# Five edits in the scan of a bidirectional RWKV-7 layer, with a new written order

## The chip, the cores and the metric

One core of a Trainium2 chip. TensorE (PE in the profile; PEld its weight loads), VectorE (DVE), ScalarE (ACT), GpSimd (POOL) and SyncE (SP, which issues the DMAs) run side by side and wait for one another through semaphores. The metric is the device time of one execution in microseconds; lower is better. The time of the kernel before is the median of three runs.

## The reference

A trunk of two layers on 512 tokens of 1024 channels. A layer is: half-step SwiGLU feed-forward, token mixer, half-step feed-forward, each followed by a layer norm. Layer 0 mixes with a neighbourhood attention; layer 1 with the bidirectional RWKV-7 mixing, the only part that the change touches:

```python
def step(state, inp):
    r_t, w_t, k_t, v_t, a_t, b_t = inp
    sa = jnp.einsum('zbhij,zbhj->zbhi', state, a_t)
    state = state * w_t[..., None, :] + sa[..., None] * b_t[..., None, :] + v_t[..., None] * k_t[..., None, :]
    return state, jnp.einsum('zbhij,zbhj->zbhi', state, r_t)

_, ys = lax.scan(step, jnp.zeros((2, B, H, N, N), f32), xs)
y = (ys[:, 0] + ys[::-1, 1]).transpose(1, 0, 2, 3)
mu = jnp.mean(y, axis=-1, keepdims=True)
var = jnp.mean(jnp.square(y - mu), axis=-1, keepdims=True)
y = ((y - mu) * lax.rsqrt(var + RW_GN_EPS)).reshape(B, S, D) * lnx_g + lnx_b
```

There are 16 heads of 64 channels (N), and two directions z, one scan each. `w` is a decay, `a` and `b` come from the normalised keys and a learned rate, `r` reads the state out. After the scan y is normalised per head, a bonus is added, it is gated and multiplied by the output matrix.

## The kernel before, in words

The two feed-forwards of layer 0, its attention and the first feed-forward of layer 1 run first, then the projections of RWKV-7, then the scan (from about 1385 to 1800 us of the profile), then the last feed-forward. All of it outside the scan is the same in both kernels.

The scan handles a *pair* of heads (128 channels, `hp` 0 to 7) at a time, and cuts the 512 tokens into eight chunks of 64. Within a chunk the recurrence becomes matrix products; a small triangular system per chunk, direction and head has to be inverted; and a *chain* of eight steps carries the 64x64 state from chunk to chunk. A *slot* n runs the chain of pair n, and beside it the preparation of the pairs n+1 to n+3 and the end of pair n-1. Each job is a generator with a one-letter name, the *threads* of `slot`, and the strings of the table `SEQ` say which thread goes on next; slots 0 to 4 share one string. The threads that matter here:

- `f0`, `f1`: `front`, one per direction. Prefix sums of the log decay (`lw` with `tri`), the exponentials `e` and `e2`, the rate `th` (a matmul of `ah` with `a2r`), and from them the factors `ar` and `bk`.
- `g0`, `g1`: `grams`, the products of `bk` and `ar` inside a chunk, masked into `xs`; ScalarE copies pieces into `qd` and `qc`, and DMAs put `ar` into `az` and `xs`. A call multiplies four chunks of two heads.
- `t0`, `t1`: `tails`, `bk` transposed to `tb`.
- `v`: `values`, eight products of the value weights `wv` with `xraw`. There is one `wv` buffer; `weigh` asks for the next pair's 512 KB when the last of the eight is issued.
- `n`: `turn`, the values transposed to tokens by rows (`vt`), once forward and once reversed.
- `i`, `k`, `j`: `invert`, `inverted`, `merge`. `invert` transposes `qd` into `qs` on VectorE and solves 31 rows of a 32x32 triangular system on GpSimd, two operations a row (`tm`, `zs`), from row 31 to row 1. `inverted` transposes the result on VectorE and sends it to `az` in eight DMAs; `merge` joins the 32x32 blocks on PE (32x32 tiles).
- `c`, `d`: `chain` (`c<-vt,xs`, `y<-vt,az`, `c<-wr,az`, `m<-vt,tb` on PE, copies on ScalarE, the decay on VectorE) and `outputs` (`y<-vt,xs`).
- `x`, `e`: `finish` (mean, variance and normalisation of y on VectorE) and `gate` (loads `bon` and `gate`, transposes y, bonus and gate on VectorE).
- `o`: `outs`, in slots 5 to 7: the first five blocks of the output product, with weights that lie in buffers of the scan that have come free (`bk`, `ar`, `az`, `wv`, `xs`).

`k.bank(tag)` takes a PSUM bank of a group: two each of `a` and `g`, one each of `p`, `c`, `m` and `y`. `wide` splits a product into two of 64 output rows. PE, ScalarE and VectorE issue in the order of the table (`manual_schedule(engines=MANUAL_SCAN)`); SP's and GpSimd's order is found by a scheduler from a model of time. In the profile an fp32 matmul is two records, a transpose one.

Of the kernel before, what the change touches and what calls it, by code (L numbers as in the profile page):

```python
# [10 lines left out]
F32 = mybir.dt.float32  # L11
# [1098 lines left out]
class Scan:  # L1110
# [13 lines left out]
    def begin(self, g2):  # L1124
# [10 lines left out]
        self.first.update(zip(("e", "e2", "th"), (ring[:, i * S : (i + 1) * S] for i in range(3))))  # L1135
# [9 lines left out]
    def open(self, pool):  # L1145

        self.pool = pool
# [3 lines left out]
        self.onesb = early.tile([P, P], F32, name="onesb")  # L1151
        unit = lambda i: (pool.tile([P, 2, 2, 4, CH], F32, name=f"xs{i}"), pool.tile([P, 2, 4, CH], F32, name=f"tb{i}"))
        units = {i: unit(i) for i in (2, 4, 3)}
        for n in ("e", "e2", "th"):
            self.place(n, [P, S], 2)
# [33 lines left out]
    def receptances(self):  # L1189
# [58 lines left out]
    def run(self, late, lead, ln):  # L1248
        with self.k.tc.manual_schedule(engines=MANUAL_SCAN):
            self.zs, self.rs, self.out = [], self.receptances(), self.outs()  # L1250
            next(self.rs)
            self.led, self.stored = [], 0
            for n in range(-2, HEADS // 2):
                if n == HEADS // 2 - 1:
                    self.early.tile([P, 56], F32, name="pad")
                    self.opened.close()
                    late.enter_context(self.k.early())
                    self.lw = self.leads(lead, ln)
                self.slot(n)
            self.ending = self.finish(HEADS // 2 - 1)  # L1260
            next(self.ending)
# [78 lines left out]
    def load(self, hp):  # L1340
# [12 lines left out]
        p.units, p.ar, p.bk = [], [], []  # L1353
# [14 lines left out]
    def front(self, hp, z):  # L1368
# [14 lines left out]
        e = tile_("e", [P, S], 2)  # L1383
        nc.scalar.activation(e, pi, AF.Exp)
# [3 lines left out]
        pa = k.bank("a")  # L1388
        self.wide(pa, p.a2[:, z, :], self.ah, True, True)
        th = tile_("th", [P, S], 2)  # L1390
        nc.scalar.activation(th, pa, AF.Tanh, scale=0.5, bias=k.col(C_A0H + z, hp))
# [15 lines left out]
        nc.vector.tensor_tensor(rt, chunks(p.r), ec, ALU.mult)  # L1407
# [18 lines left out]
    def grams(self, hp, z):  # L1426
# [5 lines left out]
        for q in range(2):  # L1432
# [4 lines left out]
            for j in range(4):  # L1437
                for h, hs in enumerate(HALF):
                    nc.tensor.matmul(pgs[h][:, j * P : (j + 1) * P], flat(bk[hs, q * 4 + j]), ar[hs, :, q * 4 + j],  # L1439
                                     start=True, stop=True)  # L1440
# [71 lines left out]
    def turn(self, hp):  # L1512
# [4 lines left out]
        for z, zs in enumerate(HALF):  # L1517
            nc.vector.memset(p.vt[zs, 0, z], 0.0)
# [3 lines left out]
        for z in range(2):  # L1522
            pv = k.bank("p")
            for t in range(NT):
                nc.tensor.transpose(pv[:, t * P : (t + 1) * P], (vr if z else p.v)[:, t * P : (t + 1) * P], k.ident)
# [8 lines left out]
    def invert(self, hp):  # L1534
# [6 lines left out]
        for s in range(31, 0, -1):  # L1541
            c0 = s // 2
            n = 16 - c0
            tm = tile_("tm", [P, 256])
            tv = tm[:, : s * n].rearrange("p (a b) -> p a b", b=n)
            nc.gpsimd.tensor_tensor(tv, qs[:, s, 0:s].rearrange("p (a o) -> p a o", o=1).broadcast_to([P, s, n]),  # L1546
                                    zs[:, s : s + 1, c0:].broadcast_to([P, s, n]), ALU.mult)
            nc.gpsimd.tensor_tensor(zs[:, 0:s, c0:], zs[:, 0:s, c0:], tv, ALU.add)  # L1548
# [44 lines left out]
    def chain(self, hp):  # L1593
# [3 lines left out]
        vt = p.vt  # L1597
# [298 lines left out]
```

## Time and profile before

| what | us |
|---|---|
| median of three runs | 2185.55 (2181.95 to 2185.77) |
| the profiled execution, its own time | 2179.1 |
| its span, first to last instruction | 2177.3 |
| PE busy | 2138.7 (98%) |
| GpSimd busy | 1392.8 (64%) |
| VectorE busy | 1052.1 (48%) |
| ScalarE busy | 954.7 (44%) |

The shares are means over stages that differ. A busy PE says little, since a matmul's record lasts until its result is written and records overlap; what tells is how far apart matmuls start, and for what PE waits. The mean granted clock of the span is 0.996 of full speed.

### The profile page before, as it was taken

Reading aid. Unit: us, or ns where it says so; the run is one execution under the profiler, and the core shown is the slowest. Engines: PE = TensorE matmul, PEld = TensorE weight load, DVE = VectorE, ACT = ScalarE, POOL = GpSimd, SP = SyncE. Lnnn points to the kernel's source line nnn. Section 1 sums busy time; section 2 is a strip of 40 time slices with the busy share of each in tenths; the row PEclk is TensorE's granted clock in tenths of the full one; section 3 lists DMA queues with packets and bytes.
Section 4 is the critical chain, followed back from the end, with each engine's and each line's share of the span. In section 5 each row is a group of like instructions: output and inputs, shape, how many; then the busy total and the mean of one; then the engine's idle time right before and its main releaser. Section 6 shows DMA issues by size and latency. Waiting matters only on the chain.

```text
span 2177.3 us, 35335 instructions
## 1 busy us (share of the span) xinstructions
PE 2138.7 (98%) x13952; PEld 1686.0 (77%) x13952; DVE 1052.1 (48%) x1526; ACT 954.7 (44%) x1675; POOL 1392.8 (64%) x1226
## 2 busy tenths in 40 slices
PE   9999999999999999999999999999999999999998
PEld 8888888888888888888888877446666568888876
DVE  3223355377333333553333569636888554333345
ACT  3333345377333333453333444537777434333333
POOL 5988855555478778578888543046767614877753
PEclk9999999999999999999999999999999999999999
DMA  6444462332244444544444553853444552444443
GB/s 210 150 155 144 142 230 97 116 114 76 91 162 140 141 145 136 212 141 142 144 137 144 198 175 125 288 172 104 133 122 128 165 190 83 150 135 141 140 165 126
DMA packets 145366, 321.47 MB, mean 148 GB/s; under 512 B 31056, under 2 KB 51152, under 8 KB 145200
## 3 DMA queue, kind: packets, MB, share of 16 engines
q1 hardware_dynamic: 145200, 319.21, 45.0%
q8 instruction: 110, 1.80, 0.3%
q14 instruction: 56, 0.46, 0.1%
HBM read 261.22 MB, written 45.88 MB: 141 GB/s over the span
## 4 chain that ended last, share of the span: by engine, by line
PE 91%; DMA 3%; DVE 2%; ACT 1%; issue 1%; POOL 1%; SPq 0%; DVEq 0%; ACTq 0%; POOLq 0%
PE bank L287 17%; PE bank L286 17%; PE bank L288 17%; PE bank L923 17%; PE a L1115 5%; PE bank L349 4%; PE g L1439 1%; PE y L1115 1%; DMA wv<-in_w_rv_dram 1%; PE bank L1306 1%; PE m L1115 1%; PE bank L677 1%; PE y L1614 1%; PE c L1607 1%; PE y L1637 1%
## 5 line engine op out<-in xcount | busy, mean ns | idle before, releaser
L277 POOL TENSOR_TENSOR w<-raw,w 128x1024 fp32r<-128x1024 f32 x198 | 485.7, 2455 | 224.4 <-ACT w L276 216.9
L286 PE MATMUL bank<-xT,w 128*128 128x512 f32 x1264 | 493.4, 390 | 0.0
L287 PE MATMUL bank<-xT,w 128*128 128x512 f32 x1264 | 492.3, 389 | 0.0
L288 PE MATMUL bank<-xT,w 128*128 128x512 f32 x1264 | 491.9, 389 | 0.0
L276 ACT ACTIVATE w<-raw 128x1024 fp32r<-128x1024 f32 x202 | 213.0, 1058 | 312.9 <-POOL ts L894 123.1
L493 DVE SCALAR_TENSOR_TENSOR ar<-bank,tmp 128x512 f32<-128x512 f32 x88 | 60.9, 692 | 570.3 <-PE bank L288 560.2
L288 PEld LDWEIGHTS bank<-xT,w 128*128 128x128 f32 x1264 | 237.3, 188 | 49.9
L286 PEld LDWEIGHTS bank<-xT,w 128*128 128x128 f32 x1264 | 237.3, 188 | 48.6
L287 PEld LDWEIGHTS bank<-xT,w 128*128 128x128 f32 x1264 | 237.4, 188 | 48.2
L923 PE MATMUL bank<-wx,an 128*128 128x512 f32 x792 | 187.5, 389 | 0.0
L923 PEld LDWEIGHTS bank<-wx,an 128*128 128x128 f32 x792 | 148.7, 188 | 31.2
L923 PE MATMUL bank<-w,ring 128*128 128x512 f32 x720 | 168.8, 390 | 1.9 <-POOL w L277 1.7
L277 POOL TENSOR_TENSOR wx<-ra,wx 128x512 fp32r<-128x512 f32 x132 | 167.0, 1291 | 3.1 <-ACT wx L276 3.1
L277 DVE TENSOR_TENSOR ring<-ar,ring 128x1024 fp32r<-128x1024 f32 x44 | 122.5, 2785 | 87.7 <-ACT ring L276 87.6
L923 PEld LDWEIGHTS bank<-w,ring 128*128 128x128 f32 x720 | 134.9, 188 | 31.1 <-POOL w L277 2.7
L491 ACT ACTIVATE tmp<-bank 128x512 f32<-128x512 f32 x88 | 52.6, 597 | 233.4 <-PE bank L288 233.2
L1546 POOL TENSOR_TENSOR tm<-qs,zs 128x126 f32<-128x126 f32 (+22 forms) x248 | 103.6, 418 | 79.3 <-issue 35.8
L1548 POOL TENSOR_TENSOR zs<-zs,tm 128x126 f32<-128x126 f32 (+22 forms) x248 | 110.9, 447 | 19.4
L276 ACT ACTIVATE wx<-ra 128x512 fp32r<-128x512 f32 x132 | 82.7, 632 | 79.3 <-PE bank L923 66.3
L277 POOL TENSOR_TENSOR ring<-raw,ring 128x1024 fp32r<-128x1024 f32 x24 | 60.1, 2515 | 78.8 <-ACT ring L276 78.8
L277 POOL TENSOR_TENSOR w<-xT,w 128x1024 fp32r<-128x1024 f32 x25 | 62.7, 2511 | 45.2 <-ACT w L276 45.2
L499 DVE TENSOR_TENSOR ar<-ar 128x256 f32<-128x256 f32 x44 | 90.3, 2052 | 1.5
(346 smaller groups left out, 3946.3 us busy)
## 6 DMA issues: line engine op xcount, KB each, us to landing
raw<-in_ffn_w_in_dram SPq DMA_DIRECT2D x176, 512.0 KB, 3.5
ra<-in_ffn_w_out_dram SPq DMA_DIRECT2D x44, 1024.0 KB, 4.9
xT<-d_late SPq DMA_DIRECT2D x29, 512.0 KB, 5.0
xT<-in_ffn_w_out_dram SPq DMA_DIRECT2D x23, 512.0 KB, 4.6
d_late<-ts SPq DMA_DIRECT2D x44, 256.0 KB, 3.0
d_late<-ra SPq DMA_DIRECT2D x44, 256.0 KB, 2.0
raw<-in_w_qkv_dram SPq DMA_DIRECT2D x16, 512.0 KB, 3.6
raw<-in_ffn_w_out_dram SPq DMA_DIRECT2D x12, 512.0 KB, 3.6
```

The costliest lines, as they stand in the source:

```text
L276: self.hi = self.nc.scalar.activation(h, raw, AF.Copy).ins
L277: self.lo = (eng or self.nc.vector).tensor_tensor(l, raw, h.bitcast(F32), ALU.subtract).ins
L286: nc.tensor.matmul(out, wh, xh, start=start, stop=False)
L287: nc.tensor.matmul(out, wh, xl, start=False, stop=False)
L288: nc.tensor.matmul(out, wl, xh, start=False, stop=stop)
L349: nc.tensor.matmul(acc[t, h], a, u[:, i, h * 512 : (h + 1) * 512], start=first and n == 0, stop=last and n == 2)
L493: nc.vector.scalar_tensor_tensor(raw[:, 3:7:3] if j else raw[:, 0:8:7], halves_of(pu), 0.5, halves_of(s), ALU.mult, ALU.mult)
L499: nc.vector.tensor_tensor(a(2), a(1), a(0), ALU.subtract)
L923: self.nc.tensor.matmul(acc, lhs, u[:, i], start=bool(first) and m == 0, stop=last and m == 2, skip_group_check=more)
L1115: self.nc.tensor.matmul(out[hs], w[:, hs], x, start=start, stop=stop)
L1546: nc.gpsimd.tensor_tensor(tv, qs[:, s, 0:s].rearrange("p (a o) -> p a o", o=1).broadcast_to([P, s, n]), zs[:, s : s + 1, c0:].broadcast_to ...
L1548: nc.gpsimd.tensor_tensor(zs[:, 0:s, c0:], zs[:, 0:s, c0:], tv, ALU.add)
```

## The change

- *Written DMA order.* From slot 0 on, SP also issues in the order in which the code asks, as the other three do; the strings of slots 0 to 7 are new.
- *Last rows on VectorE.* `invert` solves rows 31 to 5 on GpSimd; `inverted` solves rows 4 to 1 on VectorE (tile `tn`) before its transpose.
- *Values centred as they are turned.* `turn` multiplies by `centre`, the identity less 1/64 within each head, in place of a transpose. Every v has then mean zero over its head, so y has too, and `finish` drops the mean and its subtraction.
- *Both rates at once.* `front` of direction 0 makes the rates of both directions (pairs 1 to 7), each from the 64 rows of `a2r` that are not zero, on four 64x64 tiles of the array, the second into bank `p`.
- *Grams as 64x64.* A gram matmul of 64 rows and 128 columns of weights becomes two of 64 columns. In chunk 0 of the chain, whose state is zero, `c` uses the 64 rows that hold values, `y<-vt,az` is left out, and the memsets of `vt` go.
- `e` gets a column of ones on each side of a chunk (`es`), so that one operation makes `ar` in place of two.

```diff
--- before
+++ after
        "t0 v f0 v v b f0 v t1 i f0 t1 f0 v n v r b",
-    0: "x v c n g0 c c f1 f1 c v d c c c x f1 c v x c d c c v f1 c l f0 g0 f1 x c l c g0 c n v c f1 f0 g0 c d c "
-       "c n g0 d c x d g1 c g0 e g1 x c c g1 g1 v g1 c v d f1 g1 i c k t0 t0 c c k b f0 t1 t1 j c v f0 d f0 c v "
-       "c c j d f0 b",
...
+    0: "n c v x g0 c c x n c d c c c f1 x c l x f1 v c d c f1 c f1 n c f0 f1 x c g0 c c g0 g0 v c f1 v g0 c d c "
+       "c d f1 g1 c v f0 e g0 g1 t0 c c g1 b g1 c v c g1 g1 l v k i c t0 c c k f0 v c f0 v j b c t1 t1 x c c j d "
+       "d d d f0 f0",
...
 }
...
 GATES = 4
+ROWS_DVE = 4
 START_TAGS = ("k0", "iv0", "r0", "lw", "kz0", "ar0", "bk0", "a2r", "pcs")
...
         self.onesb = early.tile([P, P], F32, name="onesb")
+        self.centre = early.tile([P, P], F32, name="centre")
...
+        es = [pool.tile([P, NC, CH + 2], F32, name=f"es{i}") for i in range(2)]
+        for e in es:
+            nc.gpsimd.memset(e[:, :, 0 :: CH + 1], 1.0)
+        self.es += es * (HEADS // 2)
...
             nc.sync.dma_start(getattr(self, n), self.consts[n])
+        nc.vector.scalar_tensor_tensor(self.centre, self.onesb, -1.0 / HD, self.k.ident, ALU.mult, ALU.add)
         chunk(0)
...
     def run(self, late, lead, ln):
+        self.zs, self.rs, self.out = [], self.receptances(), self.outs()
+        self.led, self.stored = [], 0
         with self.k.tc.manual_schedule(engines=MANUAL_SCAN):
-            self.zs, self.rs, self.out = [], self.receptances(), self.outs()
             next(self.rs)
-            self.led, self.stored = [], 0
-            for n in range(-2, HEADS // 2):
+            for n in range(-2, 0):
+                self.slot(n)
+        with self.k.tc.manual_schedule(engines=MANUAL_SCAN | {mybir.EngineType.SP}):
+            for n in range(HEADS // 2):
                 if n == HEADS // 2 - 1:
...
         yield
-        e = tile_("e", [P, S], 2)
-        nc.scalar.activation(e, pi, AF.Exp)
+        ew = self.es.pop(0)
+        e = ew[:, :, 1 : CH + 1]
+        nc.scalar.activation(e, chunks(pi), AF.Exp)
         e2 = tile_("e2", [P, S], 2)
...
         yield
-        pa = k.bank("a")
-        self.wide(pa, p.a2[:, z, :], self.ah, True, True)
-        th = tile_("th", [P, S], 2)
-        nc.scalar.activation(th, pa, AF.Tanh, scale=0.5, bias=k.col(C_A0H + z, hp))
+        ways = (z,) if hp == 0 else range(2) if z == 0 else ()
+        pas = {i: k.bank("ap"[i] if len(ways) > 1 else "a") for i in ways}
+        for hs in HALF:
+            for i, pa in pas.items():
+                nc.tensor.matmul(pa[hs], p.a2[HALF[i], i, hs], self.ah[HALF[i]], start=True, stop=True)
+        for i, pa in pas.items():
+            p.th[i] = tile_("th", [P, S], 3)
+            nc.scalar.activation(p.th[i], pa, AF.Tanh, scale=0.5, bias=k.col(C_A0H + i, hp))
+        th = p.th[z]
         ar, bk = tile_(f"ar{z}", [P, 2, NC, CH]), tile_(f"bk{z}", [P, NC, 2, CH])
...
         bt, kt = bk[:, way, z, way], bk[:, way, 1 - z, way]
-        kc, ec = chunks(p.k), chunks(e)
-        if z == 0:
-            a1, a0, k1, k0, e1 = at[:, :, 1:], at[:, :, 0:1], kc[:, :, 1:], kc[:, :, 0:1], ec[:, :, : CH - 1]
-        else:
-            a1, a0, k1, k0, e1 = at[:, :, : 0 : -1], at[:, :, 0:1], kc[:, :, : CH - 1], kc[:, :, CH - 1 :], ec[:, :, 1:]
-        nc.vector.scalar_tensor_tensor(a1, k1, k.col(C_NKK, hp), e1, ALU.mult, ALU.mult)
-        nc.vector.tensor_scalar(a0, k0, k.col(C_NKK, hp), None, ALU.mult)
+        nc.vector.scalar_tensor_tensor(at[:, :, way], chunks(p.k), k.col(C_NKK, hp), ew[:, :, 2 * z : 2 * z + CH], ALU.mult, ALU.mult)
         end = 0 if z else CH - 1
-        ends = ec[:, way, end : end + 1]
+        ends = e[:, way, end : end + 1]
         for h in range(2):
...
         yield
-        nc.vector.tensor_tensor(rt, chunks(p.r), ec, ALU.mult)
+        nc.vector.tensor_tensor(rt, chunks(p.r), e, ALU.mult)
         if z == 0:
...
             for j in range(4):
-                for h, hs in enumerate(HALF):
-                    nc.tensor.matmul(pgs[h][:, j * P : (j + 1) * P], flat(bk[hs, q * 4 + j]), ar[hs, :, q * 4 + j],
-                                     start=True, stop=True)
+                for i, rows in enumerate(HALF):
+                    for h, hs in enumerate(HALF):
+                        nc.tensor.matmul(pgs[h][rows, j * P : (j + 1) * P], bk[hs, q * 4 + j, i], ar[hs, :, q * 4 + j],
+                                         start=True, stop=True)
...
         p.vt = tile_("vt", [P, NC, 2, 2, CH], 2)
-        for z, zs in enumerate(HALF):
-            nc.vector.memset(p.vt[zs, 0, z], 0.0)
         vr = tile_("vr", [P, S])
...
             for t in range(NT):
-                nc.tensor.transpose(pv[:, t * P : (t + 1) * P], (vr if z else p.v)[:, t * P : (t + 1) * P], k.ident)
+                self.wide(pv[:, t * P : (t + 1) * P], (vr if z else p.v)[:, t * P : (t + 1) * P], self.centre, True, True)
             for j in range(2):
...
         zs = self.zs.pop(0)
-        for s in range(31, 0, -1):
-            c0 = s // 2
-            n = 16 - c0
-            tm = tile_("tm", [P, 256])
-            tv = tm[:, : s * n].rearrange("p (a b) -> p a b", b=n)
-            nc.gpsimd.tensor_tensor(tv, qs[:, s, 0:s].rearrange("p (a o) -> p a o", o=1).broadcast_to([P, s, n]),
-                                    zs[:, s : s + 1, c0:].broadcast_to([P, s, n]), ALU.mult)
-            nc.gpsimd.tensor_tensor(zs[:, 0:s, c0:], zs[:, 0:s, c0:], tv, ALU.add)
         p.zs, p.qs = zs, qs
-        yield
+        for s in range(31, ROWS_DVE, -1):
+            self.eliminate(nc.gpsimd, p, s, tile_("tm", [P, 256]))
+        yield
+
+    def eliminate(self, eng, p, s, tm):
+
+        zs, qs = p.zs, p.qs
+        c0 = s // 2
+        n = 16 - c0
+        tv = tm[:, : s * n].rearrange("p (a b) -> p a b", b=n)
+        eng.tensor_tensor(tv, qs[:, s, 0:s].rearrange("p (a o) -> p a o", o=1).broadcast_to([P, s, n]),
+                          zs[:, s : s + 1, c0:].broadcast_to([P, s, n]), ALU.mult)
+        eng.tensor_tensor(zs[:, 0:s, c0:], zs[:, 0:s, c0:], tv, ALU.add)
...
         p = self.st[hp]
+        for s in range(ROWS_DVE, 0, -1):
+            self.eliminate(nc.vector, p, s, self.tile("tn", [P, 64]))
         zs, qs = p.zs, p.qs
...
         p = self.st[hp]
-        vt = p.vt
+        p.written, vt = False, p.vt
         self.py[hp] = k.bank("y").rearrange("p (h t i) -> p h t i", h=2, t=NT)
...
             for z, h in zh:
-                nc.tensor.matmul(pw[HALF[1 - z], 0, h], x[z][:, h, 0, s % 4, :], vt[:, s, z, h], start=True, stop=True)
+                r = slice(None) if s else HALF[1 - z]
+                nc.tensor.matmul(pw[HALF[1 - z], 0, h], x[z][r, h, 0, s % 4, :], vt[r, s, z, h], start=True, stop=True)
             if 0 < s < NC - 1:
...
             yield
-            for z, h in zh:
-                nc.tensor.matmul(yo[z, h], az[z][HALF[z], h, s, :], vt[HALF[z], s, z, h], start=s + h == 0, stop=False)
+            for z, h in zh if s else ():
+                assert p.written
+                nc.tensor.matmul(yo[z, h], az[z][HALF[z], h, s, :], vt[HALF[z], s, z, h], start=False, stop=False)
             yield
...
                 for z in range(2):
-                    self.nc.tensor.matmul(yo[z, h], x[z][:, h, 1, s % 4, :], p.vt[:, s, z, h], start=False, stop=s + h == NC)
+                    self.nc.tensor.matmul(yo[z, h], x[z][:, h, 1, s % 4, :], p.vt[:, s, z, h], start=s + h == 0, stop=s + h == NC)
+            p.written = True
             yield
...
-        nc.vector.tensor_reduce(sm[:, 0], y, AX.X, ALU.add)
-        nc.vector.tensor_scalar(sm[:, 0], sm[:, 0], 1.0 / HD, None, ALU.mult)
-        nc.vector.tensor_tensor(y, y, over(0), ALU.subtract)
         y2 = tile_("yh", [P, NT, 2, CH])
```

Three places in the order of instructions. First VectorE, late in a steady slot, where the inversion of one pair ends and that of the next begins (`qs<-qd` opens an inversion, `qd<-zs` closes one). Before:

```order
L1626 TENSOR_TENSOR vt<-m,pc 64x128 x2
L1422 TENSOR_TENSOR kz_12353<-kz_12128,kz_12353 128x512
L1539 STREAM_TRANSPOSE qs<-qd 128x1024
L1558 STREAM_TRANSPOSE qd<-zs 128x16x16x2
L1567 STREAM_TRANSPOSE qs<-qd 128x512
L1503 SCALAR_TENSOR_TENSOR kz_12353<-gh,cols,kz_12353 128x512
L1400 SCALAR_TENSOR_TENSOR ar_12747<-k_12361,cols,e 128x8x63
L1401 TENSOR_SCALAR ar_12747<-k_12361,cols 128x8
L1626 TENSOR_TENSOR vt<-m,pc 64x128 x2
```

and now:

```order
L1646 TENSOR_TENSOR vt<-m,pc 64x128 x2
L1564 TENSOR_TENSOR tn<-qs,zs 128x56
L1566 TENSOR_TENSOR zs<-zs,tn 128x4x14
L1564 TENSOR_TENSOR tn<-qs,zs 128x45
L1566 TENSOR_TENSOR zs<-zs,tn 128x3x15
L1564 TENSOR_TENSOR tn<-qs,zs 128x30
L1566 TENSOR_TENSOR zs<-zs,tn 128x2x15
L1564 TENSOR_TENSOR tn<-qs,zs 128x16
L1566 TENSOR_TENSOR zs<-zs,tn 128x16
L1576 STREAM_TRANSPOSE qd<-zs 128x16x16x2
L1551 STREAM_TRANSPOSE qs<-qd 128x1024
L1585 STREAM_TRANSPOSE qs<-qd 128x512
```

The transpose that closes an inversion stood behind the one that opens the next; now the eight operations of rows 4 to 1 and the closing transpose stand ahead of it.

Second PE, where a steady slot comes to the first product of a pair's values (`a<-xraw,wv`): the last rows ahead of it. Before:

```order
L1439 MATMUL g<-ar_13426,bk_13427 128x128 x8
L1614 MATMUL y<-vt,az_10636 64x64 x4
L1618 MATMUL c<-wr,az_10636 64x64 x4
L1115 MATMUL a<-tri,lw 64x128 x8
L1624 MATMUL m<-vt,tb_10628 64x64
L1624 MATMUL m<-vt,tb_10611 64x64
L1624 MATMUL m<-vt,tb_10628 64x64
L1624 MATMUL m<-vt,tb_10611 64x64
L1115 MATMUL a<-xraw,wv 64x512 x2
```

and now:

```order
L1634 MATMUL y<-vt,az_10640 64x64 x4
L1638 MATMUL c<-wr,az_10640 64x64 x4
L1116 MATMUL a<-tri,lw 64x128 x8
L1644 MATMUL m<-vt,tb_10632 64x64
L1644 MATMUL m<-vt,tb_10612 64x64
L1644 MATMUL m<-vt,tb_10632 64x64
L1644 MATMUL m<-vt,tb_10612 64x64
L1116 MATMUL a<-xraw,wv 64x512 x2
```

The rows are alike, but between the last value product of one pair and this one stand 78 matmuls before and 168 now, since the second `v` of the string moved back from the 11th to the 21st place. (The gram call that stands in the rows of before has 8 matmuls, now 16.)

Third SP, from the end of slot 5, where the output weights are asked for (`in_rw_out`). Before:

```order
L1452 DMA xs_10623<-ar_14787 64x256
L1452 DMA xs_10625<-ar_15024 64x256 x2
L1452 DMA xs_10627<-ar_15024 64x256
L1563 DMA az_10636<-qd 32x8x32 x8
L1452 DMA xs_10627<-ar_15024 64x256
L1659 DMA bk_15552<-in_rw_out_dram 128x1024
L1659 DMA az_10638<-in_rw_out_dram 128x1024
L1659 DMA ar_15553<-in_rw_out_dram 128x1024
L1721 DMA d_o<-bon 128x512
L1659 DMA az_10638<-in_rw_out_dram 128x1024
```

and now:

```order
L1739 DMA d_o<-bon 128x512
L1679 DMA xraw<-d_o 128x512
L1680 DMA bk_15582<-in_rw_out_dram 128x1024
L1679 DMA xraw<-d_o 128x512
L1680 DMA ar_15583<-in_rw_out_dram 128x1024
L1679 DMA xraw<-d_o 128x512
L1680 DMA az_10642<-in_rw_out_dram 128x1024
L1679 DMA xraw<-d_o 128x512
L1680 DMA az_10642<-in_rw_out_dram 128x1024
L1581 DMA az_10640<-qd 32x8x32 x8
L1523 DMA d_bon<-bon 128x512
L1685 DMA e_15808<-d_x 128x512
```

The eight copies `az<-qd` of the next pair's inverse stood ahead of the weights, and now stand behind four of them.

More of the change, by code (lines that the diff above doesn't have):

```diff
@@ L1134, in begin @@
         ring = self.k.ring(F32)
-        self.first.update(zip(("e", "e2", "th"), (ring[:, i * S : (i + 1) * S] for i in range(3))))
+        self.first.update(zip(("e2", "th"), (ring[:, (i + 2) * S : (i + 3) * S] for i in range(2))))
+        self.es = [ring[:, : NC * (CH + 2)].rearrange("p (c t) -> p c t", c=NC)]
+        nc.gpsimd.memset(self.es[0][:, :, 0 :: CH + 1], 1.0)
         for dst, src in ((self.ah, self.dram["ah"]), (self.tri, self.consts["tri"])):
@@ L1145, in open @@
     def open(self, pool):
+        nc = self.nc
         self.pool = pool
@@ L1151, in open @@
         self.onesb = early.tile([P, P], F32, name="onesb")
+        self.centre = early.tile([P, P], F32, name="centre")
         unit = lambda i: (pool.tile([P, 2, 2, 4, CH], F32, name=f"xs{i}"), pool.tile([P, 2, 4, CH], F32, name=f"tb{i}"))
         units = {i: unit(i) for i in (2, 4, 3)}
-        for n in ("e", "e2", "th"):
-            self.place(n, [P, S], 2)
+        es = [pool.tile([P, NC, CH + 2], F32, name=f"es{i}") for i in range(2)]
+        for e in es:
+            nc.gpsimd.memset(e[:, :, 0 :: CH + 1], 1.0)
+        self.es += es * (HEADS // 2)
+        for n, i in (("e2", 2), ("th", 3)):
+            self.place(n, [P, S], i)
         for n in ("yt", "yh"):
@@ L1352, in load @@
         p.pc = tile_("pc", [P, NC, 2], 4) if hp else tile_("pcs", [P, NC, 2])
-        p.units, p.ar, p.bk = [], [], []
+        p.units, p.ar, p.bk, p.th = [], [], [], {}
         if hp:
@@ L1662, in outs @@
             hs = slice(h * 512, (h + 1) * 512)
-            x = self.tile(("e", "e2", "th")[n % 3], [P, S], 2)
+            x = self.tile(("e2", "th")[n % 2], [P, S], 2 + n % 2)
             nc.sync.dma_start(x, rows(self.dram["x"], t)[:, hs])
```

14 rows, old and new, of the table SEQ are left out of this document.

## The prediction

> **What bounds the kernel now.** I read the chain of waits first, then PE's own waits in the scan, then a table by slot. A slot is the stretch from one head pair's first `c<-vt,xs` matmul to the next pair's; 1491.3, 1525.4, 1563.1, 1599.6, 1638.5, 1675.5, 1709.7 and 1756.8 us are those starts in the timeline. Page of the profile (chain), then what PE itself waited for between 1385 and 1805.4 us:
>
> ```profile
> PE 91%; DMA 3%; DVE 2%; ACT 1%; issue 1%; POOL 1%; SPq 0%; DVEq 0%; ACTq 0%; POOLq 0%
> ...
> PE a L1115 <- DMA wv<-in_w_rv_dram: 10.0, 5, 2.8
> PE a L1115 <- DMA ar<-in_rw_out_dram: 3.1, 1, 3.1
> PE a L1115 <- DMA bk<-in_rw_out_dram: 1.7, 1, 1.7
> ```
>
> The end is PE's; what is not PE's is mostly DMA. In the scan two loads stop PE: five reloads of `wv` (10.0 us) and the first two output weights (4.8). The slots (length, then each engine's busy time, then PEclk):
>
> ```profile
> core 0: us, PE busy (x) PEld busy (x) DVE busy (x) ACT busy (x) POOL busy (x), PEclk, DMA share, GB/s
> 1525.40:1563.10 37.70, 34.81 (x636) 25.17 (x634) 31.47 (x64) 28.61 (x79) 28.08 (x63) 1.00 0.48 127
> 1563.10:1599.60 36.50, 34.55 (x634) 25.08 (x632) 31.45 (x64) 28.55 (x79) 28.31 (x63) 1.00 0.46 125
> 1599.60:1638.50 38.90, 36.55 (x634) 26.03 (x632) 31.32 (x64) 28.59 (x79) 27.88 (x63) 0.96 0.48 122
> 1638.50:1675.50 37.00, 34.82 (x636) 25.13 (x633) 31.86 (x64) 28.63 (x79) 28.27 (x63) 1.00 0.39 104
> 1675.50:1709.70 34.20, 32.96 (x616) 24.26 (x613) 26.58 (x56) 25.71 (x73) 25.04 (x59) 1.00 0.56 155
> 1709.70:1756.80 47.10, 42.03 (x588) 22.26 (x586) 16.48 (x42) 13.38 (x38) 19.47 (x51) 0.93 0.56 184
> ...
> 1605.50:1608.80 3.30, 3.30 (x28) 1.85 (x30) 1.58 (x3) 0.28 (x1) 2.91 (x6) 0.50 0.71 212
> 1716.00:1721.50 5.50, 5.50 (x28) 1.86 (x30) 0.00 (x0) 1.00 (x3) 4.64 (x12) 0.50 0.89 342
> ```
>
> Slots 1 to 4 take 150.1 us together; slot 6 is the longest, 47.1. The last two rows are the price beside the waits: right after a stop the granted clock was 0.50, for 3.3 us in slot 3 and 5.5 us in slot 6, so 1.7 and 2.8 us of work were lost there on top.
>
> **Why `wv` is late.** The chain of waits, and the tile's own view:
>
> ```profile
> 1559.39 0.86 PE a L1115 x4
> 1562.37 5.85 DMA wv<-in_w_rv_dram
> 1568.36 1.08 PE a L1115 x4
> ...
> DMA to landing us min/median/max: 3.3/5.7/8.0
> ```
>
> There is one `wv` buffer. Its last matmul ended at 1560.25; the reload was issued at 1562.37 and landed 5.85 us later, 8.0 us after the buffer came free. PE had 78 matmuls to put between, about 6 us of work, and stood for some 2. In the new order 168 matmuls stand between the last matmul of one `wv` and the first of the next (the part on the change has the last twelve rows of each order). At the 0.08 us that the 78 took each they are 13 us; 32x32 and four-abreast ones are cheaper, so I take 10. That is over 8.0, so this wait should go, in all five places.
>
> **The PE parts.** Timeline of PE (start, time, line, count of recorded passes):
>
> ```profile
> 1565.09 1.09 PE L1115 MATMUL a<-tri,lw 128*64 128x128 f32 x16
> 1579.01 1.16 PE L1439 MATMUL g<-ar,bk 64*128 64x128 f32 x16
> 1580.93 0.27 PE L1614 MATMUL y<-vt,az 64*64 64x64 f32 x2
> ...
> 1581.21 0.23 PE L1618 MATMUL c<-wr,az 64*64 64x64 f32 x2
> 1581.37 0.66 PE L1525 MATMUL p<-ident,vr 128*128 128x128 f32 x4
> 1581.95 0.45 PE L1637 MATMUL y<-vt,xs 128*64 128x64 f32 x8
> 1635.63 0.45 PE L1614 MATMUL y<-vt,az 64*64 64x64 f32 x8
> 1635.91 0.40 PE L1618 MATMUL c<-wr,az 64*64 64x64 f32 x8
> ```
>
> An fp32 matmul is two passes, a transpose one. The fourth to seventh rows show the tiles' worth. At 1635.6 the eight passes of `y` start over 0.28 us and then the eight of `c`: two abreast, since both lines use the same two quadrants. At 1580.9 sixteen passes of the same lines start within 0.28 us: four quadrants run abreast, at no cost over two. So:
> - *Both rates at once* (slots -2 to 4, seven times): two calls of 0.86 us (a row of the chain, `a L1115 x4`) become one set on four quadrants, 0.86. Saves 0.86 a slot.
> - *Turning through `centre`*: a bank was four transposes, 0.11 us each; it becomes eight 64x128 matmuls, sixteen passes as in the `a<-tri,lw` row, 0.88. Two banks a pair: +0.9 us.
> - *Grams as 64x64*: 32 passes for 16, four abreast for two, with the same 128 columns each: 0, if they do run abreast.
> - *Chain step 0*: the four `y<-vt,az` matmuls of a zero state go: -0.15.
> - *Mode changes*: 1581.21 to 1581.37 is 0.16 us where such passes start 0.05 apart, and the four transposes take 0.58 to the next mode instead of 0.44: about 0.15 us a change. Counted in the two orders, a slot has 31 stretches of one tile size before and 25 after (grams and rates now share the 64x64 size of the chain): -0.9.
>
> Sum -1.0 us a slot. Slots 1 to 4 by PE alone: 150.1 - 8.8 (four of the `wv` waits) - 0.5 (one wait for `az`) - 1.7 (clock) - 4.0 = 135.1, 33.8 us a slot.
>
> **The inversion's loop.** GpSimd and VectorE:
>
> ```profile
> 1554.43 0.24 POOL L1546 TENSOR_TENSOR tm<-qs,zs 128x31 f32<-128x31 f32 x1 [4.84 <-issue]
> 1584.66 0.28 POOL L1546 TENSOR_TENSOR tm<-qs,zs 128x56 f32<-128x56 f32 x1
> 1587.34 0.22 POOL L1548 TENSOR_TENSOR zs<-zs,tm 128x16 f32<-128x16 f32 x1
> ...
> 1573.68 0.17 DVE L257 TENSOR_SCALAR sm<-sm 128x8 int32<-128x8 int32 x1
> 1575.30 0.61 DVE L1626 TENSOR_TENSOR vt<-m,pc 64x128 f32<-64x128 f32 x2
> 1589.60 1.25 DVE L1539 STREAM_TRANSPOSE qs<-qd 128x1024 f32<-128x1024 f32 x1
> 1590.77 1.02 DVE L1558 STREAM_TRANSPOSE qd<-zs 128x512 f32<-128x512 f32 x1
> ```
>
> All 31 rows take 33.1 us on GpSimd (1554.43 to 1587.56); it had idled 4.84 before. Rows 4 to 1 are 2.9 of it (from 1584.66). They become eight small operations on VectorE; 8 to 128 elements take 0.17 to 0.30 us, so 16 to 56 elements some 0.18 to 0.22 each, with 0.03 between: 1.8 us (not under 1.4, not over 2.4). The order matters more. Before, VectorE did the next pair's `qs` transpose (thread `i`) ahead of this pair's `zs` transpose; now `k` stands ahead of `i`. So GpSimd's next inversion waits for this one's end, through VectorE: 30.2 (rows 31 to 5) + 0.1 + 1.8 + 1.05 + 1.2 + 0.15 = 34.5 us, once a slot. The parts between are start-to-start times of the rows above. This is over PE's 33.8, so it sets slots 1 to 4: 4 x 34.5 = 138.0, or **-12.1 us**. Bounds: 33.8 a slot if GpSimd is quicker, 36 if VectorE reaches the rows 1.5 late.
>
> [...]
>
> **The other edits.** VectorE loses the row-sum, mean and subtraction of `finish`, the memsets of `vt` and the one-column `ar` operation, and gets the eight small ones: about -1 us in a slot where it is busy 31.5, worth nothing under the loop. In the last pair's `finish` PE works on anyway:
>
> ```profile
> 1784.07 7.13 PE L1306 MATMUL bank<-xs,xraw 128*128 128x512 f32 x16
> 1791.04 0.60 PE L1716 MATMUL bank<-ident,yt 128*128 128x128 f32 x4
> ```
>
> PE's sixteen passes end at 1790.9, and the transposes follow at once; a `finish` that is 1.6 us shorter brings 0 there (uncovered, it would bring those 1.6).
>
> *DMA queue in the written order.* SP now takes the DMAs in the order of the code. Its waits in slots 1 to 6:
>
> ```profile
> SPq L1452 <- ACT qc L1450: 18.8, 18, 2.3
> ```
>
> That wait for the ScalarE copies now stands ahead of `bon` and `gate` too, which VectorE needs in the same thread. I take 0 for slots 1 to 5, whose loads for the next fronts are asked for at the slot's start; up to 2.3 us a slot otherwise. At the end of slot 5 the first four output weights come before the eight `az<-qd` copies, and not behind them: the 4.8 us of slot 6 go, with its 2.8 of clock. Against that +0.6 (turning) and about 1 us (0 to 3) for the `az` copies, which land behind 3 MB (four weights, four pieces of `d_o`) at some 340 GB/s, 9 us: **-6.0**. Slot 5 loses its 1.2 us of `wv` wait and keeps the rest of the loop: **-0.5**. Slots -2 to 0: three rates -2.6, two turns +1.8, `y` and modes -0.2: **-1.0**. Slot 7 and all behind the scan: 0.
>
> Sum: -12.1 - 6.0 - 0.5 - 1.0 = -19.6 against the profiled 2179.1, 2159.5. That execution was 6.4 us under the median of the runs, 2185.55; carried over, **2166**.
>
> **Rivals.**
> - *A longer loop* (16%): VectorE is in order and over 85% busy, so `k` comes 1.5 us late; slots 36, -6.1; in slot 6, where some 27 us of PE work stand between `i` and `k` (18 output products of 0.86, two merges, the rest chain), it costs 3 more. Total -10.6, 2175. For it speaks VectorE's load, against it that the 30.2 us were measured beside a VectorE just as busy.
> - *The quadrants do not run abreast* (9%, slower): 128 columns, 32 passes or the two rates keep the array two abreast as at 1635.6. Each gram call 0.88 more, the rates 0.86: slots 1 to 4 by PE 33.8 + 4.4 = 38.2, +2.7; slots -2 to 0 +12.2; slot 5 +3.0; slot 6 -6.0. Total +11.9, 2197. It decides as soon as a gram call is over 1.2 us. The sixteen starts within 0.28 us speak against it, though at 64 columns.
> [...]
> - *The written queue makes another copy late* (10%, no change): `bon`, `gate` or `az` 2.3 us late in seven slots, 16 us, leaves -3.5, 2182.
> - *No loop, no late copy* (8%): slots 1 to 4 at 33.8, -15.0, and slot 6 at -7.0: -23.5, 2162. If slots 0 to 4 also lost 1.5 us of PE's small waits each, 2154.
>
> **How the numbers follow.** Forecast 57%, its own range 2157 to 2174. A measurement here tells 0.2%, 4.4 us, from no change. Faster: 57 + 16 + 8 = 81%; same 10%; slower 9%. The range for 8 in 10 runs from 2154 to 2183: the forecast, the longer loop, the better case and half of no change.
>
> **What would show it.** PE waits for `wv`, `bk` and `ar` gone from the scan and PEclk 1.00 in its slots; slots 1 to 4 all near 34.5, with GpSimd's idle time before each inversion filled by VectorE's eight operations and two transposes; gram calls of 32 passes in 1.1 us. Slots over 36, a gram call near 2 us, or a new DMA among PE's waits would make the forecast wrong.

## The result: slower, and the profile after

Four runs of the changed kernel took 2209.18 us in the median (2207.9 to 2211.84), four of the kernel before 2185.31: a ratio of 1.0114, 95% interval 1.0097 to 1.0132. The forecast was 2166, faster. The profiled execution took 2207.9 us, its span 2206.0, at a mean granted clock of 0.992; before it was 2177.3 at 0.996. So 28.7 us came in between the two profiled executions (23.9 between the medians).

What PE waited for between 1385 and 1834 us (us in total, times, longest):

```profile
PE a L1116 <- DMA lw<-d_lw: 11.6, 6, 3.8
PE c L1626 <- DVE vt L1646: 4.4, 8, 2.9
PE p L1734 <- DVE yt L1722: 3.8, 1, 3.8
...
PE a L1116 <- DMA wv<-in_rw_out_dram: 1.5, 1, 1.5
```

The waits for the reloads of `wv` and for `bk` and `ar` are gone, as forecast (the last row is an output weight that lands in the `wv` buffer). In their place stand loads that hardly stopped PE before: `lw` first, six times. The table by slot, with the columns of the prediction's, has slots 1, 4, 5, 6, and 7 up to the last transposes of `yt`; its last five rows are stretches at and behind stops of PE:

```profile
1527.20:1565.90 38.70, 36.42 (x716) 26.40 (x714) 30.65 (x65) 28.70 (x79) 25.47 (x55) 0.96 0.46 118
...
1641.40:1682.00 40.60, 36.33 (x716) 26.45 (x714) 30.10 (x65) 28.70 (x79) 25.34 (x54) 0.96 0.46 117
1682.00:1728.40 46.40, 39.79 (x692) 28.71 (x690) 24.58 (x57) 24.71 (x69) 22.71 (x57) 0.89 0.46 136
1728.40:1772.30 43.90, 41.06 (x599) 23.99 (x596) 13.60 (x42) 14.83 (x41) 16.05 (x41) 1.00 0.47 138
1772.30:1820.30 48.00, 40.79 (x410) 23.46 (x410) 19.77 (x47) 13.11 (x32) 9.39 (x4) 0.86 0.61 218
...
1534.10:1537.50 3.40, 3.10 (x28) 2.47 (x29) 0.59 (x3) 1.08 (x2) 2.85 (x8) 0.50 0.56 152
1650.10:1653.60 3.50, 2.83 (x26) 2.43 (x28) 0.34 (x2) 0.81 (x2) 2.96 (x7) 0.51 0.59 167
1687.70:1697.90 10.20, 8.36 (x112) 6.99 (x112) 2.94 (x6) 2.61 (x8) 8.63 (x21) 0.50 0.20 52
1790.10:1796.90 6.80, 6.13 (x49) 3.14 (x51) 0.91 (x3) 1.86 (x4) 2.34 (x1) 0.50 0.27 93
1807.20:1814.00 6.80, 6.72 (x55) 4.77 (x56) 3.07 (x8) 2.05 (x5) 0.00 (x0) 0.50 0.46 130
```

Slots 1 to 4 take 154.8 us in place of 150.1, slot 5 46.4 in place of 34.2, slot 6 43.9 in place of 47.1, slot 7 and the tail 48.0 in place of 34.8, and what lies ahead 1.8 more: +28.7. The last five rows are a second price of the stops: 30.7 us at half the clock in all.

Why `lw` is late: the timeline of SP, which issues the DMAs, from the end of slot 3 into slot 4 (start, time, line, DMA, count):

```profile
1635.75 6.15 SPq L1581 DMA_DIRECT2D az<-qd  x8
...
1642.64 0.38 SPq L1499 DMA_DIRECT2D wv<-in_w_rv_dram  x1
1643.12 0.38 SPq L1523 DMA_DIRECT2D d_bon<-bon  x1
1643.55 0.42 SPq L1379 DMA_DIRECT2D lw<-d_lw  x1
```

The chain of waits at the same place (start, time, what):

```profile
1643.55 7.18 DMA lw<-d_lw
...
1650.78 1.97 PE a L1116 x16
```

SP comes to `lw` at 1643.55, behind eight copies of the inverse, 6.15 us from the first to the last, a reload of `wv` and a store of `bon`. It lands 7.18 us later; PE's wait that ends there is the longest of the six, 3.8 us. SP had issued without a pause since 1627.98, so its earlier waits and the number of copies make this request late together. SP's two longest waits in total between 1527 and 1830 us:

```profile
SPq L1466 <- ACT vt L1640: 37.6, 9, 9.5
SPq L1739 <- DVE bon L1737: 20.0, 5, 5.1
```

Both are stores and copies of results (`xs<-ar`, `d_o<-bon`); the loads written behind them stand still, up to 9.5 us at a time.

### The profile page after: what moved, and what is told of

Same layout as the page of the kernel before. It is cut to its first block, busy times and chain, and to the rows that moved or that the text cites. A ratio compares the mean times of both kernels' runs of the same rounds, so it can differ in the third digit from the quotient of the medians.

```text
span 2206.0 us, 36515 instructions
## 1 busy us (share of the span) xinstructions
PE 2154.3 (98%) x14592; PEld 1695.9 (77%) x14592; DVE 1046.5 (47%) x1535; ACT 955.6 (43%) x1675; POOL 1370.6 (62%) x1165
## 4 chain that ended last, share of the span: by engine, by line
PE 88%; DMA 5%; DVE 2%; issue 2%; ACT 1%; POOL 1%; SPq 0%; DVEq 0%; ACTq 0%; POOLq 0%
PE bank L288 17%; PE bank L287 16%; PE bank L289 16%; PE bank L924 16%; PE bank L350 4%; PE a L1116 4%; DMA lw<-d_lw 1%; PE y L1116 1%; PE g L1453 1%; PE bank L1319 1%; PE m L1116 1%; PE bank L678 1%; PE c L1626 1%; PE bank L395 1%; PE g L1476 1%
## 5 line engine op out<-in xcount | busy, mean ns | idle before, releaser
L1564 POOL TENSOR_TENSOR tm<-qs,zs 128x126 f32<-128x126 f32 (+20 forms) x216 | 92.8, 430 | 113.4 <-issue 74.1
L1566 POOL TENSOR_TENSOR zs<-zs,tm 128x126 f32<-128x126 f32 (+20 forms) x216 | 99.7, 462 | 16.9
L278 POOL TENSOR_TENSOR w<-xT,w 128x1024 fp32r<-128x1024 f32 x25 | 63.7, 2551 | 43.9 <-ACT w L277 43.9
```

The lines of the kernel that those rows point to most:

```text
L278: self.lo = (eng or self.nc.vector).tensor_tensor(l, raw, h.bitcast(F32), ALU.subtract).ins
L1564: eng.tensor_tensor(tv, qs[:, s, 0:s].rearrange("p (a o) -> p a o", o=1).broadcast_to([P, s, n]), zs[:, s : s + 1, c0:].broadcast_to([P, s ...
L1566: eng.tensor_tensor(zs[:, 0:s, c0:], zs[:, 0:s, c0:], tv, ALU.add)
```

## The experiments

Theory Q: SP in the written order stands behind stores that wait for results, so that loads go out too late, and stops of PE bring half clock behind them, as in the last five rows of the table above. Rival S: the new order on PE, ScalarE and VectorE costs. Rival A: the arithmetic edits cost.

**e1: the queue alone undone.**

```diff
-        with self.k.tc.manual_schedule(engines=MANUAL_SCAN | {mybir.EngineType.SP}):
+        with self.k.tc.manual_schedule(engines=MANUAL_SCAN):
```

> The changed kernel, with SP's order left to the scheduler in all slots; PE, ScalarE and VectorE keep the new order, and all arithmetic edits stay. Theory Q (SP in the written order stands behind stores that wait for results, so loads needed at once are asked for late): the PE waits for lw (11.6 us in six places) go, and the half clock behind them; 25 to 45 us less than the changed kernel, 2165 to 2185. Rival S (the new order on PE, ScalarE and VectorE is what costs): 2200 to 2215, with the same VectorE waits of PE. Rival A (the arithmetic edits cost): 2200 to 2215.

Measured: 2177.68 us (2175.29 to 2180.24), ratio to before 0.9976 (0.9965 to 0.9987); span 2175.6, 30.4 less than the changed kernel. No wait for `lw` is left. Its table for slots 2, 5, 6 and 7:

```profile
1562.30:1598.00 35.70, 35.17 (x719) 25.48 (x714) 30.95 (x65) 28.80 (x79) 25.94 (x55) 1.00 0.47 130
...
1669.20:1707.90 38.70, 36.20 (x694) 25.90 (x690) 25.09 (x58) 24.78 (x69) 23.82 (x57) 1.00 0.67 198
1707.90:1748.30 40.40, 39.87 (x602) 23.39 (x598) 13.82 (x42) 14.83 (x41) 16.11 (x41) 1.00 0.51 150
1748.30:1789.90 41.60, 37.28 (x410) 22.00 (x410) 19.86 (x47) 13.04 (x32) 9.40 (x4) 0.92 0.58 200
```

A request for `lw` in SP's timeline and the matmuls that use it in PE's:

```profile
1604.39 0.38 SPq L1379 DMA_DIRECT2D lw<-d_lw  x1
...
1638.89 1.09 PE L1116 MATMUL a<-tri,lw 128*64 128x128 f32 x16
```

There are two `lw` buffers. The scheduler asks for this `lw` at 1604.39, among the copies of slot 3, when the matmuls that start at 1603.25 have read the buffer; it is used 34.5 us later, in slot 4. In the changed kernel PE stood from 1647.0 for a request that left at 1643.55. Q holds, S and A fall as causes of the loss: with the same edits and the same order on the other engines the kernel is a little faster than before. In PEclk the half clock is 3.3 us of lost work (0.08 of 41.6) against 15.0 in the changed kernel (0.04 of 38.7 and of 40.6, 0.11 of 46.4, 0.14 of 48.0). So by this estimate some 11.7 of the 30.4 us are clock, and 18.7 the stops themselves.

**e2: the written queue alone, on the old strings and the old arithmetic** (the diff of the change's `run`, nothing else).

> The kernel before with one edit: from slot 0 on SP issues in the written order; the old strings and the old arithmetic stay. Theory Q: the loads lw, gate and bon are asked for just ahead of their use here too, so PE waits for lw come in and the time grows by 10 to 40 us, 2195 to 2225. Rivals S and A: within 5 us of the kernel before, 2180 to 2190.

Measured: 2243.44 us, ratio 1.0274 (1.0248 to 1.03), +60 us: Q by sign, and more than it said. The waits of PE, then one of VectorE's:

```profile
PE c L1610 <- DVE vt L1629: 19.6, 5, 4.5
PE a L1115 <- DMA lw<-d_lw: 18.4, 5, 4.4
```

```profile
DVE bon L1720 <- DMA bon<-d_bon: 27.4, 6, 6.3
```

This last row is behind the first: VectorE waits for a `bon` that left late, and the chain's `vt` is queued behind it, so PE stands too. (In one slot VectorE stood 4.5 us until 1604.11, did two operations on `bon`, two on `xs` and then `vt`; PE stood 3.6 us until 1607.09.) With the new strings and edits the queue costs half as much, 30 us: they are an order in which it does less harm, not one in which it does good.

**e4: each `lw` asked for one front earlier**, into the buffer that is free then; SP's order is else the written one.

```diff
         lw = self.lws.pop((hp, z))
+        ahead = (hp, 1) if z == 0 else (hp + 1, 0)
+        if hp and self.has(ahead[0]):
+            self.fetch(*ahead)
```

> The changed kernel, with each front's lw asked for when the front before it begins (into the other of the two lw buffers), all else the same. Theory Q: the 11.6 us of PE waits for lw go, and what followed at half clock (up to 3.4 us of work lost a stop): 15 to 25 us less than the changed kernel, 2185 to 2195. Rivals S and A: PE stands for the next thing instead, less than 5 us are won, 2204 to 2210.

Measured: 2191.42 us (2186.73 to 2194.05), ratio 1.0032 (1.0017 to 1.0046); span 2189.4, 16.6 under the changed kernel. Slots 1 to 4 come to 35.8, 36.0, 36.5 and 36.6 us (e1: 35.7, 35.7, 35.6, 35.6). One load of 256 KB twice a slot, with the clock behind it, is more than half of the loss.

**e10: e4, with SP written in slots 0 to 4 alone and scheduled in 5 to 7.**

```diff
         with self.k.tc.manual_schedule(engines=MANUAL_SCAN | {mybir.EngineType.SP}):
-            for n in range(HEADS // 2):
+            for n in range(5):
+                self.slot(n)
+        with self.k.tc.manual_schedule(engines=MANUAL_SCAN):
+            for n in range(5, HEADS // 2):
```

> The run e4 (lw one front ahead) with SP in the written order in slots 0 to 4 alone, scheduled in slots 5 to 7. Theory Q: what e4 still lacks against e1 (14 us) are the output weights, az copies and x rows of slots 5 to 7 behind stores; 2176 to 2182. If it is the written order in slots 0 to 4: 2187 to 2192.

Measured: 2181.07 us (2178.66 to 2182.58), ratio 0.9989 (0.9979 to 0.9998); span 2179.2. So 10.2 us of span lie in SP's written order in slots 5 to 7 (in which of its transfers, no run tells), and 3.6 still separate it from e1, 2.3 of them ahead of slot 5: the price of the written order there once `lw` is asked for in time.

**e11: the stores taken out of SP's queue, not the order changed.**

```diff
-                nc.sync.dma_start(az[own, h], ar[hs, 1, ss])
-                nc.sync.dma_start(x[own, h, 0], ar[hs, 0, ss])
+                nc.scalar.dma_start(az[own, h], ar[hs, 1, ss])
+                nc.scalar.dma_start(x[own, h, 0], ar[hs, 0, ss])
```

> The changed kernel, with the sixteen copies az<-ar and xs<-ar of a slot issued by ScalarE (right behind the ScalarE copies that they stand behind anyhow) in place of SP; SP's written order is else the same. Theory Q: with the stores out of the queue the loads leave when their turn comes; PE's waits for lw fall from 11.6 to under 3 us, 2188 to 2198. Rival J (the loads are late because they are written just ahead of their use, whatever stands before them): the waits for lw stay at 8 to 12 us, 2203 to 2210. Should issuing cost ScalarE much, the chain's copies come late: over 2210.

Measured: 2220.42 us (2217.43 to 2227.22), ratio 1.0178 (1.0159 to 1.0197). PE's waits, then slot 2 of its table, then two rows of ScalarE's timeline:

```profile
PE c L1638 <- ACT wr L1630: 8.1, 11, 1.0
...
PE a L1116 <- DMA lw<-d_lw: 4.1, 3, 2.4
```

```profile
1578.70:1618.20 39.50, 36.22 (x715) 26.03 (x713) 30.70 (x64) 28.79 (x79) 25.34 (x54) 1.00 0.45 118
```

```profile
1596.36 0.47 ACTq L1466 DMA_DIRECT2D xs<-ar  x1
1596.88 0.28 ACT L1630 ACTIVATE wr<-c 128x128 f32<-128x128 f32 x1 [0.55 <-ACT qc L1464]
```

The waits for `lw` fall from 11.6 to 4.1 us, in three places in place of six: less than rival J's 8 to 12, but not under Q's 3. The request does leave earlier: for slot 2, 1.0 us ahead of the slot's start (1577.73), where in the changed kernel it left 1.2 us behind it (1567.14). But the time went up, since each issue takes ScalarE 0.47 us, and the chain's copy `wr` stands behind it: 39.5 us for this slot, where the changed kernel takes 37.1. Longer slots also give the queue more time, so the run speaks for the mechanism without measuring it, and is no way out. (SP was not free either: at the stores of `bon`, which stayed with it, it stood 103 us in all.)

**e3 and e8: the arithmetic edits on the old strings, SP scheduled.** e3 has all edits but the one on chunk 0 of the chain; e8 is e3 with `ROWS_DVE = 0`, all rows on GpSimd.

> The arithmetic edits on the old strings, SP scheduled: last rows on VectorE, turn through the centre, both rates at once, grams as 64x64, the padded e. (Chain step 0 keeps its four products with the zero state and the memsets.) Theory Q: nothing here costs; the PE parts sum to -0.9 a slot, the wv wait stays, so 2172 to 2183. Rival A: 2195 to 2215. Rival S: as Q.

> The run e3 (edits on the old strings) with all 31 rows on GpSimd again. If the rows on VectorE made e3 slow, because the old strings put the transposes that the merge needs behind them: PE's waits for qs (10.8 us in six places) go, 2174 to 2180. If another edit did it: 2186 or more.

Measured: e3 2187.83 us (2185.96 to 2191.25), ratio 1.0023 (1.0009 to 1.0038); e8 2198.18 us, ratio 1.0054 (1.0037 to 1.0071). PE's longest wait in e3, then in e8:

```profile
PE p L1599 <- DVE qs L1587: 10.8, 6, 2.1
```

```profile
PE a L1116 <- DMA wv<-in_w_rv_dram: 17.4, 5, 4.3
```

Neither theory had this. In e3 the wait for `wv` is gone by itself, because PE now stands earlier in the slot, 10.8 us in six places: the merge waits for a transpose that the rows on VectorE and the next pair's opening transpose push back. With the rows back on GpSimd (e8) that wait goes, PE comes to `wv` sooner, and waits 17.4 us for it, 7.4 more than before. A matmul saved ahead of a load that is late anyway only makes the wait longer, and the half clock comes with it: PEclk of e8's slots 1 to 4 is 0.88, 0.92, 1.00 and 0.96, where before one slot of the four had 0.96. This account fits the rows; no run takes the edits of e8 apart. So on the old strings the edits cost, 5 us in e3 and 13 in e8, and rival A holds there; with the new ones and a free queue (e1) they and the order win 5 us together.

**e5 and e6: the old strings in slot 7, and in 5 and 7, on e1** (with one `d` moved ahead, so that `y` is begun by chunk 0).

```diff
-    7: "w x x c c o o c o c o d c c c o c o c d c x c o c w o c o c c o c o c o c w c o d c o c c c c w x d c c "
-       "c d x c e x w c c c d d d",
+    7: "w x c o c c x o c o c d c c o c o c d c c o c o x w c c c o c o c d c x c w o c o c c c x o c w o c d c "
+       "c o c x d e w c c c d d d",
```

> The run with the free queue (e1), with the old string in slot 7 (one d moved ahead, so that chunk 0 is written first). Theory O (what e1 lacks against the forecast lies in the places that the new strings give to finish and gate in slots 5 and 7): PE's stop of 3.8 us for yt goes with its half clock, slot 7 and the tail take 35 to 37 us in place of 41.6, 2170 to 2174. Rival: the stop moves to another wait, 2176 to 2180.

> As e5, and slot 5 with its old string too. Theory O: slot 5 takes 34 to 35 us in place of 38.7, 2165 to 2170. Rival: slot 5's work is moved into slot 6, which grows by as much, 2170 to 2175.

Measured: e5 2171.05 us (2169.42 to 2172.55), ratio 0.9929 (0.9909 to 0.9949); e6 2174.14, ratio 0.9943 (0.9924 to 0.9962). From the tables by slot, slot 7 of e5, then slots 5 and 6 of e6:

```profile
1749.70:1784.60 34.90, 34.85 (x411) 20.76 (x410) 19.95 (x47) 13.13 (x32) 9.40 (x4) 1.00 0.60 213
```

```profile
1668.50:1706.70 38.20, 33.93 (x693) 25.04 (x688) 24.72 (x58) 25.21 (x72) 24.13 (x56) 0.96 0.48 132
1706.70:1752.80 46.10, 41.68 (x600) 23.48 (x596) 14.35 (x43) 13.86 (x39) 16.51 (x42) 0.96 0.60 193
```

Slot 7 goes from 41.6 us to 34.9, with the clock at 1.00: in the new string PE stood 3.8 us at `gate` of pair 6 (the transposes of `yt`) for VectorE's last steps on `yt`, with half clock behind it, and in the old string that wait is not there. The place of `gate` is only part of it. The chain of waits of e1 ahead of the stop, then GpSimd's timeline:

```profile
1770.91 2.37 DVE sm L262
1774.10 2.29 DVE sm L264
```

```profile
1770.89 2.36 POOL L278 TENSOR_TENSOR ring<-raw,ring 128x1024 fp32r<-128x1024 f32 x1 [2.99 <-ACT ring L277]
1774.02 2.34 POOL L278 TENSOR_TENSOR ring<-raw,ring 128x1024 fp32r<-128x1024 f32 x1 [0.78 <-ACT ring L277]
```

Two small operations of VectorE, which take 0.17 us elsewhere in this `finish`, lasted 2.4 and 2.3 us, each until the GpSimd operation that began just ahead of it had ended. Those 4.3 us too many are more than the stop. No run keeps the new string and moves GpSimd's work, so what each of the two is worth stays open. For slot 5 the rival holds: the old string wins 0.4 us there (38.6 in e5) and loses 5.3 in slot 6.

**e7 and e9: what sets slots 1 to 4 of e1 at 35.6 us.** e7 takes about 1 us a slot from PE (transposes in place of the products with `centre`, so its values are not centred); e9 is e5 with `ROWS_DVE = 2`.

> The run e1 with the values turned by transposes again, so it leaves the centring out. It tells what sets slots 1 to 4 of e1 at 35.6 us. If PE's own work: each slot 1.1 us shorter, 34.5, and 2168 to 2171 in all. If the loop of the inversion through GpSimd and VectorE: the slots stay at 35.4 to 35.7, and 2174 to 2177 in all.

> The run e5 with two rows on VectorE in place of four (GpSimd solves rows 31 to 3). In e1 and e7 VectorE works without a gap for 11 us from the last rows to the factor bk that the next gram waits for, and GpSimd has ended 1.5 us ahead of the rows. Theory V (VectorE's written work there is part of what sets 35.6 us): about 0.95 us less on VectorE a slot, slots 1 to 4 at 34.6 to 34.9, 2165 to 2168. If the loop through GpSimd sets it: slots at 35.6 or more, 2170 to 2174.

Measured: e7 2174.62 us (2173.66 to 2175.62), ratio 0.9946 (0.9927 to 0.9965); e9 2169.53 (2167.64 to 2170.37), ratio 0.9940 (0.9927 to 0.9952), between the two times expected. Slot 2 of e7, then of e9, and from the timeline of e1 GpSimd's last row operation and VectorE's first:

```profile
1561.80:1597.50 35.70, 35.02 (x692) 24.89 (x688) 30.85 (x65) 28.74 (x79) 25.93 (x55) 1.00 0.49 128
```

```profile
1561.50:1596.80 35.30, 34.98 (x716) 25.40 (x714) 29.89 (x60) 28.78 (x79) 27.17 (x58) 1.00 0.50 135
```

```profile
1585.21 0.32 POOL L1566 TENSOR_TENSOR zs<-zs,tm 128x70 f32<-128x70 f32 x1
...
1586.97 0.22 DVE L1564 TENSOR_TENSOR tn<-qs,zs 128x56 f32<-128x56 f32 x1
```

24 passes fewer a slot (692 recorded for 719) leave it at 35.7, so PE's sum alone does not set it; what e7 won, 1.7 us of span, lies outside these slots (1.0 of it in slot 6). GpSimd is done 1.4 us before VectorE takes up the rows, so its loop has slack too. Four row operations less on VectorE won 0.3 to 0.4 us in each of three slots and lost 0.5 in the fourth, not the 0.95 expected. So none of these three engines' work sets the 35.6 alone (ScalarE's was not varied); which hand-over does stays open.

## Why the prediction was wrong

**The step that failed** is "*DMA queue in the written order.* ... I take 0 for slots 1 to 5, whose loads for the next fronts are asked for at the slot's start". The request did leave near the slot's start (1643.55, slot 4 starting at 1641.4), but PE was there for it at 1647.0, and it landed at 1650.73. The step weighed neither how soon behind the request the use comes nor how long the load takes. Both stood in the trace of before: a load of `lw` took 2.8 to 4.3 us to land there (4.7 to 7.3 in the changed kernel; why longer, no run takes apart), and the row below the quoted one among SP's waits has one of 7.2 us, where the step took 2.3 at most:

```profile
SPq L1451 <- DVE vt L1626: 17.7, 4, 7.2
```

The measured price is 30.4 us of span (e1 against the changed kernel): 16.6 for `lw` (e4), 10.2 for the written order in slots 5 to 7 (e10), 3.6 for the rest, some 11.7 of all that being half clock. The rival that came nearest (10%) had the queue right but named `bon`, `gate` and `az` and not `lw`, and its 16 us left out the clock behind PE's stops, though the prediction had priced that for the stops that go. The last sign that the prediction gave, a new DMA among PE's waits, is what came.

Issuing takes time of its own: eight copies held SP for 6.15 us where the load behind them took 7.18, and each copy that e11 moved to ScalarE took 0.47 us of its time: with this many small copies that was not small, on either engine.

The other steps, against e1 where the queue hides them:

- *Waits for `wv`, `bk`, `ar`*: gone, as forecast; on the old strings (e3, e8) they stay or turn into another wait.
- *PE parts*: right in size where a row shows one. In PE's timeline of the changed kernel the 32 passes of a gram call take 1.06 us to the next start, under the 1.2 from which the rival of quadrants not abreast decides, and the 16 of a turn 0.92 (the next row starts at 1656.23), forecast 0.88. Both rates take 0.99 in e1 (1588.46 to 1589.45), forecast 0.86. The term for mode changes, -0.9, no run takes alone. The rows of the gram call and of the turn:

```profile
1584.62 1.13 PE L1453 MATMUL g<-ar,bk 64*64 64x128 f32 x32
1585.68 0.45 PE L1644 MATMUL m<-vt,tb 128*64 128x64 f32 x8
...
1655.31 1.09 PE L1116 MATMUL p<-centre,vr 128*64 128x128 f32 x16
```

- *The inversion's loop*, 34.5 us a slot, -12.1: wrong as the bound. VectorE's rows took the forecast 1.8 us (1670.97 to 1672.82 below), but GpSimd, done at 1664.25, stood idle for 11.19 us around them. With a free queue the slots are 35.6, close to the rival of a longer loop (36), though e7 and e9 show that the loop is not alone in it; slots 1 to 4 win 7.5 us, not 12.1. GpSimd and VectorE in the timeline at the end of slot 4 of the changed kernel:

```profile
1663.60 0.65 POOL L1566 TENSOR_TENSOR zs<-zs,tm 128x70 f32<-128x70 f32 x1
...
1670.97 0.22 DVE L1564 TENSOR_TENSOR tn<-qs,zs 128x56 f32<-128x56 f32 x1
...
1672.82 1.06 DVE L1576 STREAM_TRANSPOSE qd<-zs 128x512 f32<-128x512 f32 x1
...
1675.44 0.24 POOL L1564 TENSOR_TENSOR tm<-qs,zs 128x31 f32<-128x31 f32 x1 [11.19 <-issue]
```

- *Slot 6*, -6.0: near with a free queue, 47.1 to 40.4. *Slot 5*, -0.5: wrong, +4.5 in e1. The two share their work (e6): e1 needs 79.1 us for both, e6 84.3, the old kernel 81.3. Together that is -2.2 where the forecast had -6.5, so the number of slot 6 alone is in part luck.
- *Slots -2 to 0*, -1.0: +1.2 in e1. *Slot 7 and all behind*, 0: +6.8 in e1, 6.7 of it gone with the old string of slot 7 (e5). The prediction looked at the last pair's `finish` and not at the one before it.

So without the queue the range would have held (2177.68 in 2154 to 2183), but not the sum: -1.7 us of span in e1, where -19.6 stood.

## What to carry to other kernels

An order by hand for an engine that issues DMAs is a claim on time, not on sequence: for each load, ask which stores that wait for results stand ahead of it, how long its transfer takes, and put the request that far ahead. Price a stop of the matmul engine with the half clock that may follow it (in the changed kernel 3.4 to 10.2 us behind each of five stops of 1.80 us and more, none behind two of 1.48 us). And work taken away ahead of a wait is worth nothing until the wait itself is moved: the best version here is the change without its queue and with the old string in slot 7, 0.9929 of the time before (e5), or 0.9940 with two rows on VectorE (e9), which the intervals do not tell apart.

## What the runs showed of the hardware

PE's timeline at the first two late loads, and the table for the stretch behind the second (that behind the first, from 1534.10, stands above):

```profile
1534.40 0.91 PE L1116 MATMUL a<-tri,lw 128*64 128x128 f32 x6 [1.80 <-DMA lw<-d_lw]
...
1572.78 0.66 PE L1116 MATMUL a<-tri,lw 128*64 128x128 f32 x8 [1.48 <-DMA lw<-d_lw]
```

```profile
1572.80:1576.40 3.60, 3.60 (x70) 2.88 (x72) 1.88 (x8) 1.99 (x6) 3.05 (x8) 1.00 1.00 223
```

The stop of 1.80 us brought 3.4 us at half clock, the one of 1.48 us none, and the one of 1.5 us for `wv` in slot 6 none either (PEclk 1.00). At the other four long stops, in slots 4, 5 and 7 (3.79 and 3.41 us for `lw`, 2.89 for `vt`, 3.80 for `yt`), it lasted 3.5, 10.2, 6.8 and 6.8 us. But the length of the stop is not the whole of it: at 1534.10, when the clock fell, the first stop had lasted 1.5 us too. How much idle time is enough, and what sets the length of a stretch, stays open.

VectorE beside GpSimd: in the rows at e5 operations of 0.17 us lasted 2.4 and 2.3 us, until GpSimd's had ended. The trace of before has it too, in slot 7: there a `yt<-yt,sm` of VectorE that started 0.13 us behind such a GpSimd operation took 2.77 us, where it takes 0.75 on average in slots 1 to 4. What holds VectorE up there no run takes apart.
